# Two moves of work in program order in a two-layer hybrid backbone: gate-row fills one step sooner, and the opening of a seven-product FFN

## The chip, the cores and the metric

The kernel runs on one core of a Trainium2 chip. The metric is the device time of one execution in microseconds. Five engines matter here: PE (TensorE) multiplies matrices, DVE (VectorE) and ACT (ScalarE) do elementwise work, POOL (GpSimd) does slow elementwise work and fills, SP (SyncE) issues most DMAs. Each engine runs its own list of instructions in order; an instruction waits for semaphores of the others. All matrix work is fp32: each operand is split into a rounded high part and a low remainder, and each product is three matmuls (high by high, low by high, high by low).

## The reference

Two layers. Each has a mixing part and a feed-forward part on 512 latent tokens and, in layer 0, also on 256 context tokens (1024 channels):

```
z = modulate(x, norm1_g, sh1, sc1) @ w_in            # and the same for the context
au, av, bq, bk, bv, cq, ck, cv, co, cg = split_cols(z)
y_a = chunk_token_mlp(...); y_b = neighbourhood_attention(...)
h_lat, h_ctx = mlstm_bidirectional(lat_in, ctx_in, ctx_out)
x = x + g1 * (concat([y_a, y_b, h_lat * sigmoid(co)]) @ w_out)
x = x + g2 * swiglu(modulate(x, norm2_g, sh2, sc2), w_gate, w_up, w_down)
```

The mLSTM has an input gate `i` and a forget gate `f` per head, token and direction. Its running maximum and the cumulative sum of the forget gates are recurrences over tokens:

```
fcum = jnp.cumsum(fb, axis=-1)
log_intra = fcum[..., :, None] - fcum[..., None, :] + ib[..., None, :]
m_t = jnp.maximum(log_inter, jnp.max(log_intra, axis=-1))
```

## The kernel before, in words

**Mixing part.** The code of a layer is written as generators, one per strand of work: the attention head pairs B0 to B2, the mLSTM head pairs C0 to C2, the gate rows `r` (`do_Crows`, line 671), the values `v`, the modulation vectors `m`. A table of strings, `ORDERS`, says how many steps each generator takes and in what order; a step ends at a `yield`. The framework then places the emitted instructions into one list per engine, so that program order and its view of readiness set the lists; they are fixed before the program starts. In layer 0 the gate rows stand as `r:1 m:1 C0:1 r:2`: the first step of `do_Crows`, a step of modulation, a step of C0, then two more steps of `do_Crows`.

The first step of `do_Crows` spreads the gates into two padded tiles, transposes them on PE (`rowps`) and copies them out on ACT as rows `rI` and `rF` (64 partitions by 768 tokens). The second step fills two more row tiles on POOL, `rM` with 0 (line 701) and `rW` with 1 and two strips of zeros (lines 709 to 711), and runs three DVE scans that write the running maximum into `rM` (line 717). The third step runs two more scans, with `rW` as the multiplier (line 721), and a subtraction into `rI`. The fourth subtracts into `rF` (line 729), forms `rW`, `rA` and `apr`, and takes their exponentials on ACT (lines 738 to 744). Then PE transposes the rows back (`tokps`, line 759) and broadcasts `apr` (`apbps`).

Around it stand the rope products of the mLSTM (`th`, `ck`, `cq`, lines 785 to 796, with one multiply on POOL at 794), the triangular masks `s_tri` on POOL (line 850), and the large projections (`dps`, line 157), whose weights arrive by DMA as `wraw` and are split into `whi` on ACT (line 133) and `wlo` on DVE (line 134).

**Opening of layer 0's FFN.** Up and gate projections of the first layer are done by a scheme of seven products in place of eight half-size ones (`ffn_seven`, line 1417). A unit is one block of gate or up weights. The products are P1 and P2 (weights as they are), P6 and P5 (weight sums `s2`, `s1`), P7 and P4 (`b`), P3 (`s4`). Their right-hand operands are built from pairs j = 0..3 of normalised rows `hf`: P1 and P2 use `hf` itself; P6 and P5 use T2 and T1, two subtractions (`sums_12`, lines 1228 and 1229, tiles `t`) and then a split into high and low (`operands_12`, line 113 on ACT, line 114 on DVE; tiles `olh` and `oll` for j = 0, `oh` and `ol` for the others); T3, T4 and B22 come from `operands_34`. `some_steps(n)` normalises n more rows (line 1189 on DVE, line 1191 on ACT). The first two units run side by side with their operands being built, so this place is called the opening. `w1`, `w2`, `w3`, `w4` split a unit's weights (tiles `whi`, `wlo`); `X`, `Y`, `Z` are its PSUM banks (line 1314). `pin` fixes the order of the PE products as written.

Of the kernel before, what the change touches and what calls it, by code (L numbers as in the profile page):

```python
# [46 lines left out]
def tile_backbone(ctx: ExitStack, tc: tile.TileContext, A, out):  # L47
    nc = tc.nc
    te, ve, ac, gp, sp = nc.tensor, nc.vector, nc.scalar, nc.gpsimd, nc.sync
# [47 lines left out]
    def pst(pool, name="ps"):  # L97
        return pool.tile([128, 512], F32, tag="ps", name=name)
# [7 lines left out]
    def zct(name, dt=F32):  # L106
        return zc.tile([128, ZU], dt, tag="z", name=name)
# [19 lines left out]
    def wload(src):  # L127
        n = src.shape[-1]
        raw = wraw.tile([128, 1024], F32, tag="w", name="wraw")
        link(sp.dma_start(out=raw[:, 0:n], in_=src))  # L130
        hi = whl.tile([128, 1024], F32R, tag="whi", name="whi")
        lo = whl.tile([128, 1024], F32R, tag="wlo", name="wlo")
        ac.activation(out=hi[:, 0:n], in_=raw[:, 0:n], func=AF.Copy)  # L133
        ve.tensor_tensor(out=lo[:, 0:n], in0=raw[:, 0:n], in1=hi[:, 0:n].bitcast(F32), op=ALU.subtract)  # L134
        return hi, lo
# [318 lines left out]
    for l in range(2):  # L454
# [216 lines left out]
        def do_Crows():  # L671
# [13 lines left out]
            ve.tensor_scalar(out=f64v, in0=gt[:, :, :, 1, :], scalar1=0.0, scalar2=None, op0=ALU.min)  # L685
            ve.tensor_tensor(out=f64v, in0=f64v, in1=fa, op=ALU.subtract)

            def to_rows(src, name):
                t = zct(name)
                for g, (c0, n) in enumerate(((0, 4), (4, 2))):  # L690
                    ps = pst(mx, "rowps")
                    for c in range(n):
                        te.transpose(out=ps[0:64, c * 128:(c + 1) * 128], in_=src[:, c0 + c, :], identity=ident)
                    ac.activation(out=t[0:64, c0 * 128:(c0 + n) * 128], in_=ps[0:64, 0:n * 128], func=AF.Copy)
                return t
# [1 line left out]
            rI = to_rows(i64, "rI")  # L697
            rF = to_rows(f64, "rF")
            yield
            rM = zct("rM")  # L700
            gp.memset(rM[0:64, 0:768], 0.0)
            mst = tok.tile([64, 6], F32, tag="mst", name="mst")
            gp.memset(mst, 0.0)
            mla = tok.tile([64, 6], F32, tag="mla", name="mla")
            gp.memset(mla, 0.0)

            rW, rA = zct("rW"), zct("rA")
            keep = rW[0:64, 0:768].rearrange("p (c t) -> p c t", c=6)
            gp.memset(rW[0:64, 0:768], 1.0)
            gp.memset(keep[0:32, :, 0], 0.0)  # L710
            gp.memset(keep[32:64, :, 127], 0.0)
            rM3 = rM[:, 0:768].rearrange("p (c t) -> p c t", c=6)
            runs = (
                (slice(0, 6), slice(0, 768, 1), 0.0), (slice(32, 38), slice(255, None, -1), 0.0),
# [15 lines left out]
            rM, rE = rF, rM  # L730
# [466 lines left out]
        def some_steps(n):  # L1197
            for _ in range(min(n, len(steps2))):
                steps2.pop(0)()
# [4 lines left out]
        def pair_tile(wide):  # L1204
            if wide:
                t = zct("t")
                return [t[:, n1], t[:, n2]], [t[:, 0:2 * HN]]
            t = [wkt("t")[:, 0:HN] for _ in range(2)]
            return t, t

        def round_off(names, j, srcs, dst):
            hi, lo = dst
            c = 0
            for src in srcs:
                q = slice(c, c + src.shape[-1])
                split(hi[:, q], lo[:, q], src)
                c += src.shape[-1]
            for i, nm in enumerate(names):
                q = slice(i * HN, (i + 1) * HN)
                O[nm, j] = (hi[:, q], lo[:, q])  # L1220

        def out_pair():
            return [zct(nm, F32R)[:, 0:2 * HN] for nm in ("oh", "ol")]

        def sums_12(j):
            e, o = hf[2 * j], hf[2 * j + 1]
            t, _ = tsum[j] = pair_tile(j < 3)
            ve.tensor_tensor(out=t[0], in0=e[:, n2], in1=e[:, n1], op=ALU.subtract)
            ve.tensor_tensor(out=t[1], in0=o[:, n2], in1=t[0], op=ALU.subtract)

        def operands_12(j):
            dst = [O["l"][w][:, 8:10, :].rearrange("p a b -> p (a b)") for w in (0, 1)] if j == 0 else out_pair()
            round_off(("T1", "T2"), j, tsum[j][1], dst)
# [161 lines left out]
        def feed(n):  # L1395
            for _ in range(min(n, len(fill))):
                fill.pop(0)()

        units, first = [], []
# [17 lines left out]
        def ffn_seven():  # L1417

            def down(pi):
                f0, nf = FF0_PIECES[pi]  # L1420
                gh, gl = [], []
                for pr in range(f0 // 2, (f0 + nf) // 2):
                    gh += store[pr][0]
                    gl += store[pr][1]

                def gpart(g):
                    o, T = (0, 512) if g[0] == "l" else (512, 256)
                    return (lambda k: gh[k][:, o:o + T], lambda k: gl[k][:, o:o + T], T)

                cache = {}  # L1430

                def dload(k):
                    if k // 4 not in cache:
                        cache[k // 4] = wload(A["w_dn0_%d" % pi][k // 4])
                    c = (k % 4) * nf * 128
                    return [t[:, c:c + nf * 128] for t in cache[k // 4]]

                return nf, gpart, dload

            u0, u1 = first  # L1440

            some_steps(2)
            sums_12(0)
            for j in range(1, 4):
                for u in first:
                    u.prod("P1", u.X, [j])
                if j == 3:
                    for u in first:
                        u.snap1()
                for u in first:  # L1450
                    u.prod("P2", u.Y, [j])
            for u in first:
                u.w2()
                u.Z = pst(mx, "Z")
            units[2].w1()
            for j in range(4):
                if j < 3:
                    some_steps(2)
                    sums_12(j + 1)
                operands_12(j)  # L1460
                for nm, at in (("P6", "X"), ("P5", "Z")):
                    for u in first:
                        u.prod(nm, getattr(u, at), [j], start=(nm == "P5"))
            for j in range(4):
                operands_34(j)
                if j == 1:
                    u0.fin1()
                    for u in first:
                        u.snap2()
                    for u in first:  # L1470
                        u.snap5()
            u1.fin1()
            units[2].stage1(True)
            for u in first:
                u.w3()
            for u in first:
                u.prod("P7", u.X, start=False)
                u.fin22()
            u0.stage3()
            u1.stage3()  # L1480
            units[2].sums()
            units[2].w2()
            units[2].fin1()
            units[2].stage2a()
            nu = 2
            for pi in range(len(FF0_PIECES)):
                nf = FF0_PIECES[pi][1]
                if pi:
                    for i in range(nf):
                        u = units[nu + i]  # L1490
                        if i:
                            u.stage2a()
                        u.stage2b()
                        feed(1)
                        nxt = units[nu + i + 1] if nu + i + 1 < len(units) else None
                        if nxt is not None:
                            nxt.stage1()
                            nxt.sums()
                            nxt.w2()
                        u.stage3(nxt is None)  # L1500
                        if nxt is not None:
                            nxt.fin1()
                    if nxt is not None:
                        nxt.stage2a()
                    nu += nf
                nf, gpart, dload = down(pi)
                pin_d[0] = pin[0]
                if pi < len(FF0_PIECES) - 1:
                    for k in range(KD):
                        resid(dense(dload(k), nf, [gpart(g) for g in whole], mm if k % 2 == 0 else mx), k, 5, whole)  # L1510
                        if k % 4 == 1:
                            feed(1)
                    pin[0] = last_pe[0]
                else:
                    feed(len(fill))

                    def done(g, ssq):
                        norm1_begin(1, h_next, x, groups.index(g), ssq)

                    preload(AF.Sqrt)  # L1520
                    lagged(dload, nf, gpart, 5, done, *TRAIL[1], eng=ve)
# [19 lines left out]
        for pi, (f0, nf) in enumerate(FF_PIECES):  # L1541
# [32 lines left out]
            def dload(k):  # L1574
                return wload(A["w_down%d" % pi][l, k])
# [120 lines left out]
```

## Time and profile before

| what | value |
|---|---|
| median of 3 runs | 1675.41 us (1675.05 to 1676.37) |
| profiled execution: its own time | 1679.51 us |
| profiled execution: span | 1677.5 us, mean granted PE clock 0.987 |
| PE busy | 1608.3 us (96%) |
| DVE busy | 1109.3 us (66%) |
| ACT busy | 736.0 us (44%) |
| POOL busy | 150.0 us (9%) |

Times in the rows of the trace are microseconds from the start of the span. A row of the timeline has the start, the duration, the engine, the line, the operation, output from inputs, the shape and the count; a bracket at its end gives the idle time of that engine before the row, and what ended it. Durations of matmuls overlap: the distance from one start to the next is what PE spends on one. Buffer numbers are left out of the names.

### The profile page before, as it was taken

How to read it: one execution, taken by the hardware profiler on the slowest of the kernel's cores; microseconds unless marked ns; L12 is line 12 of the kernel's file. 1: busy time of each engine (PE TensorE's matmuls, PEld its weight loads, DVE VectorE, ACT ScalarE, POOL GpSimd, SP SyncE). 2: the span in 40 equal slices, each digit the busy share in tenths (PEclk: the TensorE clock that was granted, in tenths of full speed). 3: DMA queues.
4: the chain of work that ended last, by engine and by line, in shares of the span. 5: the costliest groups of instructions: out<-in, count | busy, mean ns of one | idle time of the engine just before them, and what ended most of it. 6: DMA issues, size and time to landing. Idle time of an engine off the chain costs nothing.

```text
span 1677.5 us, 26358 instructions
## 1 busy us (share of the span) xinstructions
PE 1608.3 (96%) x10536; PEld 1413.3 (84%) x10536; DVE 1109.3 (66%) x1945; ACT 736.0 (44%) x1366; POOL 150.0 (9%) x183
## 2 busy tenths in 40 slices
PE   7998998999889999999999999899989999999998
PEld 6876877878889999999999979687869988888888
DVE  4587777667887787778777774854687833333335
ACT  5564544763563333333333454545744432222235
POOL 0003013022100000000000000130143000000000
PEclk9998999999999999999999999999999999999999
DMA  8752323244223333333333323111256532323222
GB/s 305 256 164 83 103 84 98 64 136 141 76 61 107 109 113 126 114 126 121 106 126 111 122 80 117 35 64 50 71 182 196 184 122 97 101 90 99 101 71 87
DMA packets 59306, 192.91 MB, mean 115 GB/s; under 512 B 7088, under 2 KB 9008, under 8 KB 59056
## 3 DMA queue, kind: packets, MB, share of 16 engines
q1 hardware_dynamic: 53424, 170.26, 30.8%
q0 software_dynamic: 5760, 20.97, 4.1%
q8 instruction: 83, 1.36, 0.3%
q14 instruction: 39, 0.32, 0.1%
HBM read 183.87 MB, written 7.34 MB: 114 GB/s over the span
## 4 chain that ended last, share of the span: by engine, by line
PE 75%; DVE 14%; ACT 4%; DMA 3%; issue 3%; POOL 1%; DVEq 0%; SPq 0%; ACTq 0%; POOLq 0%
PE dps L157 43%; PE X L1314 10%; PE Z L1314 5%; PE wps L413 4%; PE vps L659 3%; PE Y L1314 2%; DMA wmod<-in_w_mod 2%; DVE wlo L134 2%; DVE wmod L223 1%; PE bops L553 1%; DVE junk L223 1%; PE ptps L595 1%; ACT prob L583 1%; PE bsps L553 1%; PE avps L990 1%
## 5 line engine op out<-in xcount | busy, mean ns | idle before, releaser
L133 ACT ACTIVATE whi<-wraw 128x1024 fp32r<-128x1024 f32 (+2 forms) x178 | 180.9, 1017 | 342.8 <-PE dps L157 224.3
L134 DVE TENSOR_TENSOR wlo<-wraw,whi 128x1024 fp32r<-128x1024 f32 (+2 forms) x178 | 211.2, 1187 | 130.7 <-ACT whi L133 116.3
L1126 DVE SCALAR_TENSOR_TENSOR x<-dps,modT,x 128x512 f32<-128x512 f32 (+1 forms) x240 | 137.6, 602 | 84.1 <-PE dps L157 79.6
L157 PE MATMUL dps<-gh,whi 128*128 128x512 f32 (+1 forms) x576 | 171.4, 343 | 1.8 <-DVE x L1126 1.7
L157 PE MATMUL dps<-gl,whi 128*128 128x512 f32 (+1 forms) x576 | 170.6, 342 | 0.8 <-DVE gl L114 0.8
L157 PE MATMUL dps<-gh,wlo 128*128 128x512 f32 (+1 forms) x576 | 170.5, 341 | 0.0
L223 DVE SCALAR_TENSOR_TENSOR wmod<-wmod,c_all 128x1024 f32<-128x1024 f32 x96 | 120.9, 1260 | 29.3 <-DMA wmod<-in_w_mod 28.9
L157 PE MATMUL dps<-ll,whi 128*128 128x512 f32 x336 | 135.7, 404 | 0.2 <-DVE ll L114 0.2
L157 PE MATMUL dps<-lh,wlo 128*128 128x512 f32 x336 | 135.3, 403 | 0.0
L157 PE MATMUL dps<-lh,whi 128*128 128x512 f32 x336 | 134.8, 402 | 0.0
L157 PE MATMUL dps<-h2lh,whi 128*128 128x512 f32 (+1 forms) x336 | 128.0, 384 | 0.0
L157 PE MATMUL dps<-h2ll,whi 128*128 128x512 f32 (+1 forms) x336 | 128.0, 384 | 0.0
L157 PE MATMUL dps<-h2lh,wlo 128*128 128x512 f32 (+1 forms) x336 | 127.9, 384 | 0.0
L157 PEld LDWEIGHTS dps<-gh,whi 128*128 128x128 f32 x576 | 98.4, 189 | 16.5 <-DVE x L1126 2.9
L157 PEld LDWEIGHTS dps<-gl,whi 128*128 128x128 f32 x576 | 97.4, 188 | 15.2 <-DVE gl L114 1.9
L157 PEld LDWEIGHTS dps<-gh,wlo 128*128 128x128 f32 x576 | 97.4, 188 | 13.4
L113 ACT ACTIVATE whi<-s 128x512 fp32r<-128x512 f32 x66 | 39.4, 627 | 102.8 <-PE dps L157 75.5
L157 PE MATMUL dps<-ch,whi 128*128 128x256 f32 x256 | 74.9, 292 | 8.5 <-ACT bv L528 5.4
L113 ACT ACTIVATE whi<-wraw 128x1024 fp32r<-128x1024 f32 x44 | 46.4, 1055 | 74.1 <-PE dps L157 68.0
L157 PE MATMUL dps<-ch,wlo 128*128 128x256 f32 x256 | 74.4, 291 | 2.9 <-DVE wlo L134 2.9
L157 PEld LDWEIGHTS dps<-lh,whi 128*128 128x128 f32 x336 | 64.2, 191 | 14.7 <-issue 1.3
L157 PEld LDWEIGHTS dps<-ll,whi 128*128 128x128 f32 x336 | 64.2, 191 | 14.5 <-issue 1.7
(408 smaller groups left out, 3884.5 us busy)
## 6 DMA issues: line engine op xcount, KB each, us to landing
wmod<-in_w_mod SPq DMA_DIRECT2D x56, 512.0 KB, 3.7
wraw<-in_w_seven SPq DMA_DIRECT2D x44, 512.0 KB, 3.3
wmod<-in_w_mod POOLq DMA_DIRECT2D x40, 512.0 KB, 3.8
wraw<-in_win_blk SPq DMA_DIRECT2D x34, 512.0 KB, 3.6
wraw<-in_w_out SPq DMA_DIRECT2D x23, 512.0 KB, 3.4
wraw<-in_w_dn SPq DMA_DIRECT2D x22, 512.0 KB, 3.3
wraw<-in_w_up SPq DMA_DIRECT2D x21, 512.0 KB, 3.3
wraw<-in_w_gate SPq DMA_DIRECT2D x20, 512.0 KB, 3.3
```

What stands on the lines that cost most here:

```text
L113: ac.activation(out=hi, in_=src, func=AF.Copy)
L133: ac.activation(out=hi[:, 0:n], in_=raw[:, 0:n], func=AF.Copy)
L134: ve.tensor_tensor(out=lo[:, 0:n], in0=raw[:, 0:n], in1=hi[:, 0:n].bitcast(F32), op=ALU.subtract)
L157: m = te.matmul(out=ps[:, 0:T], lhsT=wt[:, c], rhs=(flo if wh else fhi)(k), start=(k == 0 and wi == 0), stop=(k == nk - 1 and wi == 2),)
L223: ve.scalar_tensor_tensor(out=wraw.tile([128, D], F32, tag="w", name="junk") if t < ts[-1] else raw, in0=raw, scalar=1.0, in1=c_all[:, t, ...
L413: m = te.matmul(out=ps[:, 0:T], lhsT=wt[:, cs_], rhs=(flo if wh else fhi)(k), start=(k == 0 and wi == 0), stop=(k == KD - 1 and wi == 2))
L553: m = te.matmul(*args, **kw)
L583: ac.activation(out=pt[:, 0:n], in_=sps[:, 0:n], func=AF.Exp, bias=nm, accum_out=sm_)
L595: te.transpose(out=tps[:, i * 128:(i + 1) * 128], in_=pt[:, i * 128:(i + 1) * 128], identity=ident)
L659: te.matmul(out=vps[i][:, 0:408], lhsT=tokslice(nm, k, i), rhs=wt[:, cs], start=(k == 0 and wi == 0), stop=(k == KD - 1 and wi == 2))
L1126: ve.scalar_tensor_tensor(out=xs, in0=ps, scalar=modT[:, row * 8 + k, g[3]:g[3] + 1], in1=xs, op0=ALU.mult, op1=ALU.add)
L1314: m = te.matmul(out=ps[:, 0:HN], lhsT=wt[:, c], rhs=O[op, j][wh], start=(start and j == 0 and wi == 0), stop=(j == 3 and wi == 2), skip_gr ...
```

## The change

In `do_Crows` the tiles `rM` and `rW` are allocated and filled on POOL before the first `yield`, thus in the first step instead of the second. In `ffn_seven`, T1 and T2 of pair 0 are written ahead of the weight-sum splits of the first two units; rows 2 and 3 and the subtractions of pair 1 move up with them. The split of the third unit's plain weights moves from before the loop to its pass j = 2.

```diff
             ve.tensor_tensor(out=f64v, in0=f64v, in1=fa, op=ALU.subtract)
 
+            rM = zct("rM")
+            gp.memset(rM[0:64, 0:768], 0.0)
+            rW = zct("rW")
+            keep = rW[0:64, 0:768].rearrange("p (c t) -> p c t", c=6)
+            gp.memset(rW[0:64, 0:768], 1.0)
+            gp.memset(keep[0:32, :, 0], 0.0)
+            gp.memset(keep[32:64, :, 127], 0.0)
+
             def to_rows(src, name):
...
             yield
-            rM = zct("rM")
-            gp.memset(rM[0:64, 0:768], 0.0)
             mst = tok.tile([64, 6], F32, tag="mst", name="mst")
...
-            rW, rA = zct("rW"), zct("rA")
-            keep = rW[0:64, 0:768].rearrange("p (c t) -> p c t", c=6)
-            gp.memset(rW[0:64, 0:768], 1.0)
-            gp.memset(keep[0:32, :, 0], 0.0)
-            gp.memset(keep[32:64, :, 127], 0.0)
+            rA = zct("rA")
...
                 for u in first:
                     u.prod("P2", u.Y, [j])
+            some_steps(2)
+            sums_12(1)
+            operands_12(0)
             for u in first:
                 u.w2()
                 u.Z = pst(mx, "Z")
-            units[2].w1()
             for j in range(4):
-                if j < 3:
+                if 0 < j < 3:
                     some_steps(2)
                     sums_12(j + 1)
-                operands_12(j)
+                if j:
+                    operands_12(j)
+                if j == 2:
+                    units[2].w1()
                 for nm, at in (("P6", "X"), ("P5", "Z")):
```

No instruction is added or dropped; the lists of the engines change at three places: the gate rows of layer 0, the opening, and the gate rows of layer 1. Line numbers of the changed kernel are larger by 2 behind line 721, and by 7 behind the FFN's opening.

POOL at the gate rows of layer 0 (`f` is the padded forget-gate tile, `th` the rope product, `s_tri` and `s_sb` the masks). Before:

```order
L677 MEMSET f_1238 128x384
L794 ISA
L794 TENSOR_TENSOR th<-th,cst 128x512 x2
L850 AFFINE_SELECT s_tri<-s_sb 128x768 x2
L701 MEMSET rM 64x768
L709 MEMSET rW 64x768
L850 AFFINE_SELECT s_sb<-s_sb 128x768
L710 MEMSET rW 32x6
L711 MEMSET rW 32x6
```

With the change:

```order
L677 MEMSET f_1238 128x384
L689 MEMSET rM 64x768
L692 MEMSET rW 64x768
L693 MEMSET rW 32x6
L694 MEMSET rW 32x6
L796 ISA
L796 TENSOR_TENSOR th<-th,cst 128x512 x2
L852 AFFINE_SELECT s_tri<-s_sb 128x768 x2
L852 AFFINE_SELECT s_sb<-s_sb 128x768 x2
```

The four fills stand directly behind the fill of `f`, ahead of both rope products and all masks.

DVE in the opening, from the subtractions of pair 0 (`t_4864`) on; `wlo_4908` and `wlo_4915`, with the change `wlo_4917` and `wlo_4924`, are the low halves of the two units' weight sums, `wlo_4926` is that of the third unit. Before:

```order
L1228 TENSOR_TENSOR t_4864<-hf_4542 128x384
L1189 SCALAR_TENSOR_TENSOR hf_4544<-x2_4148,a2_230,rb_4858 128x256
L1229 TENSOR_TENSOR t_4864<-hf_4543,t_4864 128x384
L1189 SCALAR_TENSOR_TENSOR hf_4545<-x3_4149,a2_230,rb_4858 128x256
L1189 SCALAR_TENSOR_TENSOR hf_4546<-x4_4150,a2_230,rb_4858 128x256
L114 TENSOR_TENSOR wlo_4915<-s2_4829,whi_4914 128x512
L114 TENSOR_TENSOR wlo_4915<-s1_4828,whi_4914 128x512
L114 TENSOR_TENSOR wlo_4926<-wraw_4921,whi_4925 128x1024
L1228 TENSOR_TENSOR t_4933<-hf_4544 128x384
L114 TENSOR_TENSOR oll_4541<-t_4864,olh_4540 128x768
```

With the change:

```order
L1230 TENSOR_TENSOR t_4864<-hf_4542 128x384
L1191 SCALAR_TENSOR_TENSOR hf_4545<-x3_4149,a2_230,rb_4858 128x256
L1231 TENSOR_TENSOR t_4864<-hf_4543,t_4864 128x384
L1230 TENSOR_TENSOR t_4911<-hf_4544 128x384
L114 TENSOR_TENSOR wlo_4917<-s1_4821,whi_4916 128x512
L1231 TENSOR_TENSOR t_4911<-hf_4545,t_4911 128x384
L114 TENSOR_TENSOR oll_4541<-t_4864,olh_4540 128x768
L114 TENSOR_TENSOR wlo_4924<-s2_4829,whi_4923 128x512
L114 TENSOR_TENSOR wlo_4924<-s1_4828,whi_4923 128x512
L1191 SCALAR_TENSOR_TENSOR hf_4546<-x4_4150,a2_230,rb_4858 128x256
```

The split `oll` of pair 0 now stands ahead of the second unit's low halves; the third unit's low half has left this place and follows the split of pair 2. On ACT, `olh` moves likewise ahead of the second unit's two high halves and of the third unit's.

DVE at the gate rows of layer 1; `wlo_10657` is the low half of a projection's weights, `th` and `cq` belong to the rope products, `rM`, `rF`, `rI`, `rW`, `rA` are the gate rows. Before, from that split to the first scan of 768 tokens:

```order
L580 TENSOR_REDUCE nm_10422<-bsps_10413 128x1
L134 TENSOR_TENSOR wlo_10657<-wraw_10654,whi_10656 128x1024
L584 RECIPROCAL sum_10425<-sum_10425 128x1
L580 TENSOR_REDUCE nm_10430<-bsps_10414 128x1
L584 RECIPROCAL sum_10433<-sum_10433 128x1
L791 SCALAR_TENSOR_TENSOR cq_9869<-th_10471,cq_9869 128x512
L793 STREAM_SHUFFLE th_10471<-cq_9869 128x512
L785 SCALAR_TENSOR_TENSOR cq_10283<-dps_10484,small_673,cq_10283 128x511
L795 TENSOR_TENSOR cq_9869<-cq_9869,cst_96 128x512
L787 SCALAR_TENSOR_TENSOR cq_10283<-dps_10484,small_673,cq_10283 128x511
L796 TENSOR_TENSOR cq_9869<-th_10471,cq_9869 128x512
L717 SCALAR_TENSOR_TENSOR rM_10519<-rF_10378,rI_10367 6x768
```

With the change, from the subtraction into `rI` (the scans stand ahead of it) to that split:

```order
L729 TENSOR_TENSOR rI_10373<-rI_10373,rF_10384 64x768
L795 STREAM_SHUFFLE th_10518<-cq_10283 128x512
L731 TENSOR_TENSOR rF_10384<-rM_10367,rF_10384 64x768
L797 TENSOR_TENSOR cq_10283<-cq_10283,cst_96 128x512
L734 COPY mla_10527<-rF_10384 6x6
L735 COPY mla_10527<-rF_10384 6x6
L798 TENSOR_TENSOR cq_10283<-th_10518,cq_10283 128x512
L739 TENSOR_TENSOR rW_10369<-rF_10384,mst_10525 64x768
L741 TENSOR_TENSOR rA_10529<-rI_10373,mla_10527 64x768
L745 TENSOR_TENSOR apr_10548<-mst_10525,mla_10527 64x6
L134 TENSOR_TENSOR wlo_10657<-wraw_10654,whi_10656 128x1024
```

Before, the split stood ahead of all scans; now it stands behind the whole chain of gate rows, and the scans of 768 tokens stand ahead of the rope products of `cq`.

## The prediction

> **What bounds the kernel now.** I read the page first, its busy shares and its chain of waits, then the list of PE's waits, then windows around the longest waits inside the changed places, then the rows there.
>
> ```profile
> PE 1608.3 (96%) x10536; PEld 1413.3 (84%) x10536; DVE 1109.3 (66%) x1945; ACT 736.0 (44%) x1366; POOL 150.0 (9%) x183
> PE 75%; DVE 14%; ACT 4%; DMA 3%; issue 3%; POOL 1%; DVEq 0%; SPq 0%; ACTq 0%; POOLq 0%
> PE dps L157 <- ACT bv L528: 5.4, 1, 5.4
> PE tokps L759 <- DVE rI L727: 5.1, 1, 5.1
> PE X L1314 <- ACT olh L113: 3.0, 1, 3.0
> ```
>
> PE is busy for 96% and carries 75% of the chain: the time moves only where PE stops waiting or runs faster. Of its waits (total, number, longest), the second, third and seventh largest totals lie in the three places whose lists change. A wait costs more than itself, as the granted clock shows (columns: window; PE busy, PEld, DVE, ACT, POOL; clock; DMA share; GB/s):
>
> ```profile
> 122.00:166.00 44.00, 36.82 (x279) 30.97 (x279) 34.33 (x65) 23.19 (x52) 11.80 (x16) 0.91 0.23 70
> 152.00:157.00 5.00, 4.61 (x18) 4.36 (x19) 4.93 (x13) 4.67 (x11) 0.14 (x2) 0.50 0.36 107
> 166.00:203.00 37.00, 36.94 (x300) 30.92 (x300) 25.75 (x54) 17.21 (x45) 1.07 (x2) 0.97 0.34 105
> 462.00:468.00 6.00, 5.28 (x15) 4.88 (x16) 6.00 (x13) 4.81 (x10) 0.00 (x0) 0.50 0.00 0
> 468.00:500.00 32.00, 28.94 (x157) 27.03 (x157) 28.06 (x49) 19.75 (x34) 1.67 (x3) 0.99 0.18 52
> 1091.00:1096.00 5.00, 5.00 (x19) 4.23 (x18) 4.92 (x9) 2.85 (x5) 0.00 (x0) 0.50 0.54 160
> ```
>
> After each of the three long waits PE runs at half clock for 5 to 6 us, which loses some 2.6 us more. Which gap brings that on? Rows with gaps between:
>
> ```profile
> 439.34 0.39 PE L157 MATMUL dps<-ch,wlo 128*128 128x256 f32 x1 [1.74 <-DVE wlo L134]
> 437.00:444.00 7.00, 4.01 (x29) 3.60 (x30) 7.00 (x10) 6.43 (x12) 2.01 (x3) 1.00 0.21 75
> 255.68 0.45 PE L870 MATMUL ups<-av,kt 128*64 128x65 f32 x8 [2.32 <-POOL av L843]
> 260.00:264.00 4.00, 4.00 (x15) 3.38 (x15) 1.91 (x5) 2.94 (x12) 1.42 (x3) 0.54 0.06 25
> 1225.52 1.47 PE L827 MATMUL sps<-cq,ck 64*128 64x128 f32 x16 [3.22 <-DVE cq L796]
> 1225.00:1230.00 5.00, 4.48 (x28) 4.05 (x29) 5.00 (x6) 2.56 (x5) 5.00 (x5) 0.66 0.25 77
> ```
>
> A gap of 1.74 us, with two smaller ones near it, left the clock at 1.00. A gap of 2.32 us (and a shorter one behind it) and one of 3.22 us halved it.
>
> **Layer 0's gate rows.** The fills cost the same wherever they stand; the term is what waits for them.
>
> ```profile
> 136.81 2.28 POOL L850 TENSOR_SCALAR_AFFINE_SELECT s_tri<-s_sb 128x768 f32<-128x768 f32 x2 [3.65 <-ACT s_sb L836]
> 139.04 0.73 POOL L701 MEMSET rM<- 64x768 f32 x1
> 139.80 2.97 DVE L717 TENSOR_TENSOR_SCAN rM<-rF,rI 6x768 f32<-6x768 f32 x2 [2.25 <-POOL rM L701]
> 149.98 0.94 DVE L729 TENSOR_TENSOR rF<-rM,rF 64x768 f32<-64x768 f32 x1
> 151.02 0.84 ACT L741 ACTIVATE rM<-rM 64x768 f32<-64x768 f32 x1 [0.30 <-DVE rF L729]
> 151.77 0.57 ACT L528 ACTIVATE bv<-dps 128x512 f32<-128x512 f32 x1
> 152.39 0.58 PE L157 MATMUL dps<-ch,whi 128*128 128x256 f32 x1 [5.36 <-ACT bv L528]
> 129.75 0.85 ACT L694 ACTIVATE rF<-rowps 64x512 f32<-64x512 f32 x2
> 130.53 0.74 DVE L793 STREAM_SHUFFLE th<-cq 128x512 f32<-128x512 f32 x1
> ```
>
> The chain is: masks, fill, scans, subtraction into rF, exponential of rM on ACT; bv stands behind that exponential in ACT's list, and PE waits for bv. With the fills standing far ahead, the scans wait only for rF's copy (129.75 + 0.85) and for the shuffle ahead of them on DVE (130.53 + 0.74): they start at about 131.3, 8.5 us sooner. Walking the new DVE list with these durations (three scans 4.2, two scans 3.5, two rope operations 1.3 and one weight split 1.2 among them, rI's subtraction 0.9) brings rF's subtraction to 143.1 in place of 149.98; rM's exponential starts there.
>
> What is late next: ACT's new list has rM's exponential, two softmax exponentials with their read-outs, rW's exponential and only then the scaled probabilities. They are ready at about 146.5, and PE, with the products ahead of their transposes (ptps) done, is there at 143.4: a wait of 3.1 us. Three smaller waits come on the way: 0.85 for the rows rF (1.52 before), 1.25 for a rope addition of ck that now stands behind a reciprocal, and 0.5 at bops. Waits before, 122 to 166: 1.52 + 0.23 + 5.36 = 7.1; after: 0.85 + 1.25 + 0.5 + 3.1 = 5.7. That gains 1.4. Half clock before cost 2.65 (152.39 to 157.7) and again about 0.95 at 165.9 to 167.8, together 3.6. If the gap of 3.1 halves the clock again (2.6 lost, as behind the 3.05 and the 5.36), the place gains 1.4 + 3.6 − 2.6 = 2.4; if not, 5.0. Being nearest to the gaps of 3.05 and 3.22, it most likely does, though the stretch behind 3.22 was shorter, some 4 us with 2 lost: I take **2.7** of 2.4 to 5.0. The rope of cq and the weight split that slip behind the scans are hidden: that weight's products start long after 142.2, where its low half lands. Without that cover they would cost up to their 1.2.
>
> The Trainium skill, page "TensorE: Matmul & The Clock Gate", section "Part 1: The HAM clock gate", says that the clock halves after at least one idle window of about 3.4 us, the windows running freely. By that no gap of about 3 us would halve it, and the place would gain the 5.0. The rows above speak against it (3.05, 3.22 halved); it enters as a rival.
>
> **The opening.** Now:
>
> ```profile
> 459.54 1.28 DVE L114 TENSOR_TENSOR wlo<-s,whi 128x512 fp32r<-128x512 f32 x2
> 460.80 1.22 DVE L114 TENSOR_TENSOR wlo<-wraw,whi 128x1024 fp32r<-128x1024 f32 x1
> 461.46 0.83 ACT L113 ACTIVATE olh<-t 128x768 fp32r<-128x768 f32 x1
> 462.41 0.95 DVE L114 TENSOR_TENSOR oll<-t,olh 128x768 fp32r<-128x768 f32 x1
> 465.01 0.95 DVE L114 TENSOR_TENSOR ol<-t,oh 128x768 fp32r<-128x768 f32 x1
> 462.35 0.69 PE L1314 MATMUL X<-olh,whi 128*128 128x384 f32 x1 [3.05 <-ACT olh L113]
> 463.41 0.69 PE L1314 MATMUL X<-oll,whi 128*128 128x384 f32 x1 [0.38 <-DVE oll L114]
> 475.80 0.96 DVE L114 TENSOR_TENSOR ol<-t,oh 128x768 fp32r<-128x768 f32 x1 [1.08 <-ACT oh L113]
> 478.08 1.21 DVE L114 TENSOR_TENSOR wlo<-wraw,whi 128x1024 fp32r<-128x1024 f32 x1
> 484.17 0.44 PE L1314 MATMUL X<-oh,wlo 128*128 128x384 f32 x1 [1.10 <-DVE wlo L114]
> ```
>
> PE waits 3.05 for olh, which stands on ACT behind two units' splits, then 0.38 for oll, then runs at half clock to 468.4. With the splits behind it, olh starts once pair 0's subtractions are done (one at 458.1 in the new list), at 459.0, and ends at 459.8; oll ends at about 461.0. So pair 0 starts 2.4 us sooner. But DVE is never idle from 443 to 473, and moving rows does not make it shorter: its new list gives ol of pair 1 a start at 464.65 (465.01 before), of pair 2 at 466.0 (467.68), of pair 3 at 468.5. PE's pair 0 (12 products, 0.174 each) is over at 463.1, and PE waits about 2.5 us in two pieces for pair 1. Then it follows, pair 3 ending at about 471.9 in place of 474.0.
>
> Late next: ACT takes the banks Z, then a third-stage weight's high half, then the oh that DVE awaited for 1.08 at 475.80. All this moves up by some 0.6 to 1.5, so DVE loses most of its 1.08 wait, and the low half at 478.08, for which PE waits behind it, lands about 0.9 sooner. From there to the end of the opening DVE works 28.06 of 32 us and each PE wait (the 1.10 at 484.17 the largest) is for DVE, so both keep the shift. Bounds: none, if PE halves its clock again here and pair 3 ends where it did; 2.1, if all of pair 3's lead survives. The gaps (0.7, 1.0, 1.4, 1.1) are of the size of those at 437 to 444 that left the clock alone. I take **0.9**. The third unit's split, two passes later, costs nothing: its first products stand behind pair 3 and all six later waits; ahead of pair 3's ol, it takes the 1.14 that the earlier place gives back.
>
> **Layer 1's gate rows.**
>
> ```profile
> 1065.42 1.79 DVE L795 TENSOR_TENSOR ck<-ck,cst 128x512 f32<-128x512 f32 x1
> 1078.27 1.74 DVE L717 TENSOR_TENSOR_SCAN rM<-rF,rI 6x768 f32<-6x768 f32 x1
> 1089.54 0.95 DVE L727 TENSOR_TENSOR rI<-rI,rF 64x768 f32<-64x768 f32 x1
> 1090.55 0.90 PE L759 MATMUL tokps<-cst,rI 64*128 64x64 f32 x6 [5.13 <-DVE rI L727]
> ```
>
> Here too the scans move up, into DVE's idle time at 1061 to 1064 and behind it, and rI ends at about 1083.3 in place of 1090.5. PE's list has tokps six products earlier, so it comes there at 1080.4 and waits 2.95. But the split wlo_10657, which was done at 1071.7, now stands behind rA and apr and lands at about 1089.9; PE has six high-half products ready (1.2) and then waits some 3 us for it. From 1089.9: two products 0.35, two groups of tokps 0.8, apbps 1.4, then 43 products of 0.231 and 21 of 0.12, 12.4: 1105.0, where before was 1106.36. At full clock the gain is 1.4. With half clock behind the second gap, 2.6 lost, it is −1.2. Between, because the half-clock stretch behind the first gap falls mostly into the second wait and costs nothing there: **0.5**.
>
> **Sum.** 2.7 + 0.9 + 0.5 = 4.1. From the profiled execution, 1679.51 (span 1677.5 and 2.0 around it), that is 1675.4; it stands 4.1 above the median shown, 1675.41, so the changed kernel's median would be **1671.3**. What lies between the places stays as it is: PE has no wait to speak of from 166 to 203 (36.94 of 37), none worth naming from 500 to 950, and the waits at 227 to 260 follow work that shifts along. A difference under 0.2%, 3.35 us, is not told from no change here.
>
> **The rivals.** (1) *The waits only move* (0.28): layer 0 keeps its gain of 1.4 in waits, but the half clock comes back in both places, and the opening stays bound by DVE: 2.4 + 0.4 − 1.2 = 1.6, 1673.8. For: new gaps of 2.95 to 3.1 in place of old of 5.1 to 5.4; DVE without slack in the opening. Against: 255.68 is the shortest gap with that effect, and layer 1's first gap is mostly covered.
> (2) *No new half clock* (0.2): 5.0 + 1.3 + 1.4 = 7.7, 1667.7. The window that the Trainium skill's page states would give this; the 3.05 and 3.22 rows speak against it, the 1.74 for gaps that come out shorter than I walked.
> (3) *The late low half makes it slower* (0.12): in layer 1, wlo_10657 behind the gate chain decides PE. It breaks even when it lands at 1091.3; rope operations next to POOL's multiply take up to 1.79 (at 1065.42) where one alone in layer 0 took 0.69, and several of them stand ahead of it, so it can land at 1093, costing 1.7, and with half clock 2.6 more: −4.3. If the same pushing back of rope work behind scans makes layer 0's masks late (sps is released by cq, as at 1225.52, waiting 3.22), its 2.7 goes as well: with the opening's 0.9 the sum is −3.4, 1678.8.
> (4) *The change does not reach PE* (0.05): other rows on DVE hold the scans; 0, 1675.4.
>
> **How the numbers follow.** My forecast has 0.35, with a range of its own from 1669.5 to 1673. Range: 1666.8 (rival 2 with 0.9 more) to 1677.2 (rival 3 by half its distance), leaving about 2 in 10 outside. Faster by over 3.35: most of the forecast (0.25 of 0.35), rival 2 (0.2) and some of rival 1 (0.07): 0.52. Slower by over 3.35: rival 3, 0.12. Within: 0.36.
>
> **What would show it.** Right: POOL's fills ahead of its rope product in both layers; scans in layer 0 at 131 to 132; PE's wait for bv gone and one of about 3 for prob at ptps, half clock behind it; in the opening olh near 459.0, PE waiting at pair 1 instead of pair 0; in layer 1 a wait for rI near 3 and one for wlo_10657. Wrong: scans of layer 0 later than 135, a wait for bv or cq over 3, layer 1's trps later than 1106.4 less the shift ahead of it, or a clock below 0.9 in 462 to 468.

## The result, and the profile after

| kernel | median | ratio to before (95% interval) |
|---|---|---|
| before, timed beside it | 1676.37 us (1675.05 to 1678.03, 5 runs) | |
| changed | 1684.63 us (1682.81 to 1689.69, 5 runs) | 1.0053 (1.0042 to 1.0065) |
| changed, timed once more (e5 below) | 1684.13 us, before 1677.76 us | 1.0040 (1.0027 to 1.0054) |

The change makes the kernel slower by some 6 to 9 us. The forecast was 1671.3 us, with a range up to 1677.2: sign and size were wrong. One of the twelve executions of e2 below ran at a granted clock of 0.556 and took 2595.02 us; e2's figures leave it out.

The busy row of the changed kernel's page (span 1681.8 us, own time 1684.63):

```profile
PE 1609.5 (96%) x10536; PEld 1413.3 (84%) x10536; DVE 1112.4 (66%) x1945; ACT 734.7 (44%) x1366; POOL 150.9 (9%) x183
```

The two rows of its list of PE's waits that answer to those of before (total, number, longest):

```profile
PE ptps L595 <- ACT prob L585: 10.5, 7, 5.5
...
PE tokps L761 <- DVE rI L729: 3.5, 1, 3.5
```

The three old waits are gone from the top or shorter: bv no longer stands there, rI went from 5.1 to 3.5. In their place ptps waits 10.5 us in seven waits for the scaled probabilities (4.3 in five before). To see where time is lost, the same product is found in both profiled executions and its starts are compared (`sps` is a product of the mLSTM that needs the rope product of `cq`; `ptps` and `trps` are transposes):

| PE's product, place | before, us | changed, us | shift |
|---|---|---|---|
| first ptps in attention's second pair, layer 0 | 97.67 | 97.36 | −0.3 |
| sps, in the gate rows of layer 0 | 134.18 | 136.96 | +2.8 |
| last product Y ahead of the opening | 458.96 | 462.68 | +3.7 |
| first dps behind the opening | 499.15 | 501.56 | +2.4 |
| tail of layer 0's FFN (last Z) | 950.79 | 951.78 | +1.0 |
| trps behind the gate rows of layer 1 | 1106.36 | 1109.40 | +3.0 |

So layer 0 lost, the opening gained 1.3, and layer 1 lost. Part of the first loss is a half clock at 99 to 102 that the change did not touch (last section), and the FFN between 502 and 951 took 449.6 to 452.5 us from one profile to another with the same PE list, so single profiles tell the place, not the amount to a microsecond; the amounts come from timed experiments.

**Layer 0.** Rows of the changed kernel's timeline around the gate rows, of POOL, of DVE, of ACT and of PE:

```profile
132.44 3.20 POOL L796 TENSOR_TENSOR th<-th,cst 128x512 f32<-128x512 f32 x1 [9.81 <-ACT kt L818]
142.88 1.67 POOL L852 TENSOR_SCALAR_AFFINE_SELECT s_sb<-s_sb 128x768 f32<-128x768 f32 x2
132.17 1.73 DVE L719 TENSOR_TENSOR_SCAN rM<-rF,rI 6x768 f32<-6x768 f32 x1
134.51 1.67 DVE L719 TENSOR_TENSOR_SCAN rM<-rF,rI 6x256 f32<-6x256 f32 x1
138.25 4.01 DVE L723 TENSOR_TENSOR_SCAN rF<-rW,rF 6x768 f32<-6x768 f32 x2
142.29 0.65 DVE L725 COPY mst<-rM 6x5 f32<-6x5 f32 x1
142.95 0.80 DVE L726 COPY mst<-rM 6x3 f32<-6x3 f32 x1
143.90 1.46 DVE L729 TENSOR_TENSOR rI<-rI,rF 64x768 f32<-64x768 f32 x1
146.42 0.94 DVE L731 TENSOR_TENSOR rF<-rM,rF 64x768 f32<-64x768 f32 x1
147.45 0.84 ACT L743 ACTIVATE rM<-rM 64x768 f32<-64x768 f32 x1 [6.89 <-DVE rF L731]
150.49 0.89 ACT L585 ACTIVATE prob<-prob,sum 128x256 f32<-128x256 f32 x2
151.04 1.11 PE L595 MATMUL ptps<-cst,prob 128*128 128x128 f32 x4 [5.54 <-ACT prob L585]
179.49 0.66 PE L595 MATMUL ptps<-cst,prob 128*128 128x128 f32 x4 [0.67 <-ACT prob L585]
190.85 0.39 PE L157 MATMUL dps<-ch,whi 128*128 128x256 f32 x1 [0.76 <-ACT bk L528]
```

The scans do start 7.6 us sooner (132.17 for 139.80). But the subtraction into rF comes only 3.6 us sooner, and the probabilities behind its exponential make PE wait 5.54, as long as bv did. The windows (PE busy, PEld, DVE, ACT, POOL; clock; DMA share; GB/s) of the places whose windows of before stand in the prediction:

```profile
122.00:166.00 44.00, 35.88 (x281) 28.99 (x280) 36.88 (x68) 25.56 (x61) 13.43 (x14) 0.92 0.14 47
151.00:157.00 6.00, 5.96 (x18) 4.62 (x18) 3.91 (x6) 4.92 (x10) 0.00 (x0) 0.51 0.26 87
166.00:203.00 37.00, 35.51 (x296) 29.21 (x295) 22.32 (x43) 15.27 (x38) 0.00 (x0) 1.00 0.36 108
462.00:468.00 6.00, 3.66 (x18) 2.77 (x17) 6.00 (x13) 5.99 (x12) 0.00 (x0) 1.00 0.07 28
1085.00:1099.00 14.00, 11.17 (x45) 8.79 (x44) 10.29 (x13) 6.09 (x11) 3.46 (x4) 0.51 0.34 99
```

Half clock stands again behind the long wait, at 151 to 157, and at 166 to 203, where PE was busy 36.94 of 37 before, it is now 35.51: the two last PE rows above are new waits there.

**Layer 1.** PE's rows:

```profile
1083.46 0.56 PE L761 MATMUL tokps<-cst,rI 64*128 64x64 f32 x6 [3.46 <-DVE rI L729]
...
1087.28 0.58 PE L157 MATMUL dps<-ch,whi 128*128 128x256 f32 x1 [1.27 <-ACT bk L528]
...
1090.49 0.80 PE L157 MATMUL dps<-lh,wlo 128*128 128x512 f32 x1 [1.56 <-DVE wlo L134]
...
1092.77 2.67 PE L774 MATMUL apbps<-apr,selp 64*128 64x6 f32 x12
...
1109.40 0.81 PE L489 MATMUL trps<-cst,ck 128*128 128x128 f32 x6
```

Three waits follow each other, 3.46, 1.27 and 1.56, and the last row of the windows above shows the price: 14 us at half clock, against the 5 of before.

**The opening** answers to the forecast. PE's waits:

```profile
463.69 0.44 PE L1316 MATMUL X<-olh,whi 128*128 128x384 f32 x1 [0.67 <-ACT olh L113]
464.82 0.44 PE L1316 MATMUL X<-oll,whi 128*128 128x384 f32 x1 [0.69 <-DVE oll L114]
468.09 0.44 PE L1316 MATMUL X<-oh,whi 128*128 128x384 f32 x1 [1.08 <-ACT oh L113]
469.41 0.45 PE L1316 MATMUL X<-ol,whi 128*128 128x384 f32 x1 [0.88 <-DVE ol L114]
482.04 0.45 PE L1316 MATMUL X<-oh,wlo 128*128 128x384 f32 x1 [1.76 <-DVE wlo L114]
```

The wait of 3.05 at pair 0 became 0.67, pair 1 now waits 1.96 in two pieces, and the clock at 462 to 468 is 1.00.

### The profile page after: what moved, and what is told of

It is laid out like the page before. It is cut to its first block, busy times and chain, and to the rows that moved or that the text cites. A ratio compares the mean times of both kernels' runs of the same rounds, so it can differ in the third digit from the quotient of the medians.

```text
span 1681.8 us, 26366 instructions
## 1 busy us (share of the span) xinstructions
PE 1609.5 (96%) x10536; PEld 1413.3 (84%) x10536; DVE 1112.4 (66%) x1945; ACT 734.7 (44%) x1366; POOL 150.9 (9%) x183
## 4 chain that ended last, share of the span: by engine, by line
PE 75%; DVE 15%; ACT 5%; issue 2%; DMA 2%; POOL 1%; DVEq 0%; SPq 0%; ACTq 0%; POOLq 0%
PE dps L157 44%; PE X L1316 10%; PE Z L1316 5%; PE wps L413 4%; PE vps L659 3%; PE Y L1316 2%; DVE wlo L134 2%; DMA wmod<-in_w_mod 2%; DVE wmod L223 1%; PE bops L553 1%; DVE junk L223 1%; PE ptps L595 1%; ACT prob L583 1%; PE avps L992 1%; PE bsps L553 1%
## 5 line engine op out<-in xcount | busy, mean ns | idle before, releaser
L157 PEld LDWEIGHTS dps<-lh,wlo 128*128 128x128 f32 x336 | 64.3, 191 | 15.7 <-DVE wlo L134 2.3
```

Source lines behind the costliest of these rows:

```text
L157: m = te.matmul(out=ps[:, 0:T], lhsT=wt[:, c], rhs=(flo if wh else fhi)(k), start=(k == 0 and wi == 0), stop=(k == nk - 1 and wi == 2),)
```

## The experiments

Theory A: both moved gate rows cost time, each for a reason of its own place, and the opening gives a little back. Rivals: one of the two places alone carries the loss, or the opening does. Four kernels take the change apart.

**e1_rows_only**: the early fills in both layers, the opening as before.

```diff
+            rM = zct("rM")                        # in do_Crows, ahead of the first yield,
+            gp.memset(rM[0:64, 0:768], 0.0)       # with the fills of rW, as in the change
...
             for u in first:                       # in ffn_seven, as before
                 u.w2()
                 u.Z = pst(mx, "Z")
             units[2].w1()
```

> Only the early fills of rM and rW (both layers); the opening as before. Theory A (the gate rows lose: in layer 0 the scans now run beside GpSimd's rope multiply and masks and PE waits 5.5 us for prob; in layer 1 a weight split stands behind the whole gate chain and PE stays at half clock for some 13 us): 5 to 9 us slower than before. Theory B (chance half-clock stretches elsewhere make the difference): within 1.5 us of before in the median. Theory C (the opening is what loses): 4 us faster, as forecast for the rows.

Measured: 1684.98 us beside 1677.96, ratio 1.0044 (1.0032 to 1.0056). Within the intervals the whole loss stands in the gate rows.

**e2_opening_only**: the change's hunk in ffn_seven alone, the fills as before.

```diff
+            some_steps(2)
+            sums_12(1)
+            operands_12(0)
             for u in first:
...
-            units[2].w1()
...
+                if j == 2:
+                    units[2].w1()
```

> Only the changed opening; the gate rows as before. Theory A: 0.5 to 2 us faster than before, with PE waiting less than 1 us for olh and no half clock at 459 to 470. Theory B: within 1.5 us of before. Theory C: 4 to 9 us slower.

Measured: 1678.92 us beside 1677.96, ratio 1.000 (0.999 to 1.0011). No gain that can be told. From the last Y ahead of the opening to the first dps behind it, profiles of kernels with the old opening show 40.0 to 40.6 us (seven of them); with the new one 38.9 in three (changed, e2, e10) and 40.6 to 40.7 in three others (e5, e6, e7). The last section shows the clock that goes with it.

**e3_rows_layer0** and **e4_rows_layer1**: the early fills in one layer only, the opening as before.

```diff
+            if not last:          # e3; e4 has: if last
+                rM = zct("rM")
+                gp.memset(rM[0:64, 0:768], 0.0)
...
             yield
+            if last:              # e3; e4 has: if not last
+                rM = zct("rM")
...
```

> Early fills in layer 0 alone. Theory A: 1.5 to 4 us slower than before, with a wait of 5 us or more for prob at ptps and half clock behind it. Forecast as it was made: 2.7 us faster. Theory B: within 1.5 us.

> Early fills in layer 1 alone. Theory A: 2.5 to 5 us slower than before, half clock from about 1083 to 1099. Forecast as it was made: 0.5 us faster; its slower rival: 1.7 to 4.3 slower. Theory B: within 1.5 us.

Measured: e3 1680.60 us, 1.0016 (1.0006 to 1.0025); e4 1681.13 us, 1.0022 (1.0013 to 1.0032), both beside 1677.96. By the ratios layer 0 loses about 2.7 us and layer 1 about 3.7, together 6.4, where e1 lost 7.4 with an interval of 5.4 to 9.4. No rival holds. Layer 1's chain alone, PE's rows of e4:

```profile
1083.97 0.87 PE L772 MATMUL tokps<-cst,rI 64*128 64x64 f32 x6 [3.46 <-DVE rI L740]
...
1093.26 2.67 PE L785 MATMUL apbps<-apr,selp 64*128 64x6 f32 x12
```

And the window behind that wait:

```profile
1087.00:1099.00 12.00, 10.58 (x42) 8.21 (x41) 8.79 (x13) 5.55 (x11) 2.50 (x3) 0.50 0.34 99
```

The wait is the same 3.46, and the half clock about as long.

**e5_change_again**: the changed kernel once more, beside the next three.

> The changed kernel once more, beside the two that are built on it, on the same chip. Theory A (two mechanisms in the gate rows, layer 0 and layer 1): 6 to 9 us slower than before, as e1. Theory B (chance half-clock stretches): anything within 3 us.

Measured: 1.0040 (1.0027 to 1.0054).

**e6_masks_late**: does POOL's work beside the scans make rF late? Layer 0's first masks are emitted one step later; in the lists only POOL's four mask rows move.

```diff
-            s_tri = [[masked(su, zct("s_tri"), 0) for su in s_sb], None]
+            late = p == 0 and not last
+            if not late:
+                s_tri = [[masked(su, zct("s_tri"), 0) for su in s_sb], None]
             yield
+            if late:
+                s_tri = [[masked(su, zct("s_tri"), 0) for su in s_sb], None]
```

> The changed kernel, but layer 0's first masks (GpSimd, line 852) are written one step later, so that GpSimd does them after the scans; nothing else moves on any engine. Theory A1 (the scans run slow because GpSimd's masks run beside them): the two scans into rF take 3.5 us again in place of 4.0, the copies mst 0.15 each in place of 0.65 and 0.80, rI's subtraction 0.95 in place of 1.46; PE's wait for prob at ptps falls by some 2 us and the time by 1 to 3 us against the changed kernel. Theory A2 (only the order of the lists counts): no change in the scans and the wait.

Rows of e6, DVE, then PE:

```profile
138.74 3.52 DVE L723 TENSOR_TENSOR_SCAN rF<-rW,rF 6x768 f32<-6x768 f32 x2
142.29 0.16 DVE L725 COPY mst<-rM 6x5 f32<-6x5 f32 x1
142.46 0.16 DVE L726 COPY mst<-rM 6x3 f32<-6x3 f32 x1
142.77 0.95 DVE L729 TENSOR_TENSOR rI<-rI,rF 64x768 f32<-64x768 f32 x1
144.78 0.94 DVE L731 TENSOR_TENSOR rF<-rM,rF 64x768 f32<-64x768 f32 x1
149.40 0.84 PE L595 MATMUL ptps<-cst,prob 128*128 128x128 f32 x4 [2.58 <-ACT prob L585]
```

With no mask beside them the two scans take 3.52 in place of 4.01, the copies 0.16 in place of 0.65 and 0.80, rI's subtraction 0.95 in place of 1.46, and PE's wait falls from 5.54 to 2.58. That POOL's masks stretched the chain is shown. In the profiles the move gives back layer 0's loss: from PE's arrival at the rowps of 126 us to its arrival at the product of layer 0's tail that waits 0.57 for whi (last section), the five profiles with layer 0's fills early, the masks and the softmax in their old places, show 313.4 to 315.2 us, the six with the fills late 307.6 to 310.3, and e6 shows 310.7. In the time it does not show: 1684.71 us, 1.0035 (1.0021 to 1.0049), against 1.0040 of e5, with five executions of each. So what part of layer 0's timed loss the masks carry stays open, and even without them the early fills win nothing in that one profile of the stretch.

**e7_split_first_l1**: is layer 1's loss the order in which the weight split, the gate chain and PE's tokps stand? One word of the changed kernel's table moves.

```diff
-    ("B0:1 C1:1 B0:1 v:2 B0:2 v:1 B0:1 C0:1 r:1 B0:1 C1:1 C0:1 r:4 B1:1 C0:3 ...
+    ("B0:1 C1:1 B0:1 v:2 B0:2 v:1 B0:1 C0:1 r:1 B0:1 C1:1 C0:1 B1:1 r:4 C0:3 ...
```

> The changed kernel, but in layer 1 the step of the attention pair B1 that holds the late weight split is written ahead of the gate rows' last four steps. The split then stands among the scans on DVE, not behind the chain. Theory A (the late split starves PE and keeps it at half clock): the half clock from 1083 to 1099 is gone or short, and the time is 3 to 7 us below the changed kernel. Theory A3 (layer 1 loses because rI itself is late and tokps waits for it): the wait for rI stays near 3.5 and the time within 1.5 us of the changed kernel.

Measured: 1672.45 us beside 1677.76, 0.9968 (0.9955 to 0.998): 11.7 us faster than the changed kernel timed beside it (1684.13), more than the 3 to 7 of theory A, and faster than before. The window of layer 1's gate rows in the kernel before:

```profile
1070.00:1111.00 41.00, 35.87 (x214) 29.85 (x213) 29.76 (x44) 17.11 (x35) 7.14 (x10) 0.92 0.23 71
```

In the changed kernel:

```profile
1070.00:1111.00 41.00, 34.71 (x182) 28.66 (x182) 26.88 (x39) 15.04 (x30) 5.61 (x5) 0.83 0.20 61
```

In e7:

```profile
1070.00:1111.00 41.00, 41.00 (x317) 33.93 (x318) 32.27 (x56) 20.06 (x45) 12.66 (x15) 1.00 0.25 74
```

Its row of tokps:

```profile
1096.49 0.59 PE L761 MATMUL tokps<-cst,rI 64*128 64x64 f32 x6
```

In e7 PE never stops in these 41 us and the clock stays at 1.00. The splits stand among the scans on DVE (`wlo` at 1073.26 and 1081.89 in place of 1089.22), and tokps stands later in PE's list: PE comes to it at 1096.5, where it came to it and waited at 1080.0 in the changed kernel. Of these 16.5 us 1.6 are e7's lag from earlier, so some 15 us of ready products stand ahead of tokps, and the gate chain is done when PE comes. The one word moves both, the split and tokps; no run moves the late split alone.

**e8_softmax_first_l0**: can the same be done in layer 0? Early fills in layer 0 alone, masks late as in e6, and the softmax put ahead of rF's subtraction on DVE and of the gate exponentials on ACT.

```diff
-  ... C0:1 r:2 B0:1 m:1 r:1 m:1 B0:2 r:1 C0:1 ...
+  ... C0:1 r:2 B0:1 m:1 m:1 B0:2 r:1 r:1 C0:1 ...
+            if not last:
+                after(i, soft[0])     # rF's subtraction behind the softmax's reciprocal
...
+            if not last:
+                after(i, soft[1])     # rE's exponential behind the scaled probabilities
```

> Early fills in layer 0 alone, masks late as in e6, and the softmax of the attention block ahead of the exponentials of the gate rows on ACT and ahead of rF's subtraction on DVE. Layer 1 and opening as before. Theory A (in layer 0 PE waits for prob because the gate rows' exponentials stand ahead of it): the wait of 5.5 at ptps falls below 2 us, and the kernel is 1 to 5 us faster than before. Rival: the wait turns up at tokps or at the masks, and the time is within 1.5 us of e3.

Measured: 1678.43 us, 1.0005 (0.9997 to 1.0014). By the ratios most of e3's loss (1.0016) is back, though the intervals overlap, but nothing is won, and neither expectation holds in full: ptps still waits 3.21 (5.50 in e3), and a new wait of 0.58 for POOL's av stands at 164. Late masks and the softmax's place are moved together here, so what each gives back is not told apart.

**e9_order_alone**: the kernel before with the word of e7 moved and nothing else.

```diff
-  ... C0:1 r:4 B1:1 C0:3 ...
+  ... C0:1 B1:1 r:4 C0:3 ...
```

**e10_l1_early_split_first_opening**: e9 with the early fills in layer 1 alone (as in e4) and the new opening (as in e2). **e11_l1_early_split_first**: e10 with the old opening, thus e9 and the fills alone.

```diff
-  ... C0:1 r:4 B1:1 C0:3 ...
+  ... C0:1 B1:1 r:4 C0:3 ...
+            if last:
+                rM = zct("rM")
...
+            some_steps(2)                         # e10 alone, with the rest of e2's hunk
```

> The kernel before with one word of layer 1's table moved, the projection's step ahead of the four gate-row steps; all fills late, opening as before. Theory A (what pays in layer 1 is where the weight split and tokps stand; the early fills only made the scans' start possible): the scans still stand behind POOL's late fill, but tokps stands later in PE's list, so that the 5.1 us wait for rI at 1090.5 shrinks to 0 to 2 us and its half clock goes: 3 to 6 us faster, ratio 0.9965 to 0.998. Theory B (the gain needs both, the early fills and the order): the gate chain ends as late as before and PE meets it at another product: within 1.5 us of the kernel before, ratio 0.999 to 1.001.

> Early fills in layer 1 alone, with the projection's step ahead of the gate-row steps there, and the changed opening; layer 0's fills as before. Theory A (layer 0's early fills cost 2.7 us wherever layer 1 stands): e7 less that loss, 0.9968 less 0.0016: 0.995 to 0.9957, some 7.5 us faster than before. Rival (the losses do not add; half clock falls elsewhere): the ratio of e7 again, 0.9955 to 0.998.

> As the kernel with early fills and the new order in layer 1 and the changed opening, but with the opening as before. Theory A (the opening is worth nothing that these times can tell, as timed alone at 1.000): within 0.001 of that kernel. Rival (the opening gains the 1.2 us that two profiles show): 0.0007 above it.

Measured, beside before at 1677.09: e9 1673.35 us, 0.998 (0.9971 to 0.9989); e10 1668.17 us, 0.9942 (0.993 to 0.9955); e11 1669.10 us, 0.995 (0.9938 to 0.9963). So the order alone gains 3.7; the early fills in layer 1, a loss of 3.7 in the old order, gain another 4 in the new one (e11 against e9); and layer 0's early fills, by which e7 differs from e10, cost about 4 (0.9968 against 0.9942; the 2.7 of e3 lies within these intervals). PE's rows of e9:

```profile
1091.70 0.58 PE L759 MATMUL tokps<-cst,rI 64*128 64x64 f32 x6
1093.80 0.58 PE L759 MATMUL tokps<-cst,rA 64*128 64x64 f32 x6 [1.51 <-ACT rA L740]
```

The windows of e9 behind that wait:

```profile
1095.00:1099.00 4.00, 4.00 (x20) 3.01 (x21) 3.03 (x4) 2.98 (x10) 1.64 (x3) 0.60 0.29 87
1099.00:1103.00 4.00, 4.00 (x37) 3.03 (x37) 0.00 (x0) 1.48 (x3) 2.12 (x5) 0.55 0.47 175
```

PE's rows of e10:

```profile
1092.27 0.59 PE L772 MATMUL tokps<-cst,rI 64*128 64x64 f32 x6
1092.69 0.54 PE L772 MATMUL tokps<-cst,rA 64*128 64x64 f32 x6
...
1093.44 1.45 PE L785 MATMUL apbps<-apr,selp 64*128 64x6 f32 x12
```

With the fills late (e9) the chain ends just too late: no wait for rI, but 1.51 for the exponential of rA, and half clock behind it. Theory A had the half clock gone; over 1070 to 1111 the clock is the 0.92 of before, and what e9 saves is waiting, 1.51 for 5.13. In the kernel before, the split was not late (done at 1071.7), so this gain is put down to tokps' place. With the fills early (e10) there is no wait at all. e10 is the best version found, 9 us under the kernel before. Whether its opening adds anything over e11 is not told apart, 1 us of medians with intervals that overlap.

## Why the prediction was wrong

**Layer 1, +0.5 forecast, −3.7 measured (e4).** The walk of DVE's list was right: rI at 1083.3 (1083.46), the low half at 1089.9 (it released PE at 1090.49). The step that failed is "because the half-clock stretch behind the first gap falls mostly into the second wait and costs nothing there". The waits were shorter than one clock stretch but came in a row, and the clock stayed at 0.51 from 1085 to 1099: apbps took 2.67 for the 1.4 of the sum, and from apbps to trps it was 16.6 us for 13.8. That is the 4.4 by which trps missed 1105.0 (1109.40): 0.6 in the low half, 1.1 in the products and tokps behind it, 2.8 from apbps on, each rounded. The lower bound named, −1.2, had the right side but priced one stretch of 5 us where 14 came.

**Layer 0, +2.7 forecast, −2.7 measured (e3).** The scans' start was right: 131.3 forecast, 132.17 with the 1.0 that the head had slipped. "Walking the new DVE list with these durations" failed. The durations came from rows where the rope product on POOL and two of the four masks were over when the scans began; moved ahead, the scans run beside the rope product, and what follows runs beside all four masks. Beyond the forecast rows: 0.5 for the short scan (1.67 for 1.17), 0.5 for the two scans into rF, 0.7 for the second copy (0.80 for 0.13), 0.5 for rI. rF's subtraction came at 146.42 for 143.1, 2.3 late beside the head's 1.0. A second slip lies behind it: the text let rM's exponential start at 143.1, where the subtraction of 0.94 only begins; it started at 147.45. So the probabilities were 4.5 later than forecast, PE itself 2.1, and the wait at ptps was 5.54 for 3.1; e6 shows it as 2.58 with the masks away. The trace of before had the sign. Its last two masks already ran beside the short scan (1.17, where layer 1 of the same trace has 0.68) and, the last of them from 142.50 to 143.43, beside the first copy (0.65, where e6 has 0.16):

```profile
140.41 1.82 POOL L850 TENSOR_SCALAR_AFFINE_SELECT s_sb<-s_sb 128x768 f32<-128x768 f32 x1
142.80 0.65 DVE L723 COPY mst<-rM 6x5 f32<-6x5 f32 x1
```

Two waits of 0.67 and 0.76 behind 166, where the text said that what lies between the places stays as it is, make up 1.4 more: with all named waits the place has 9.3, where 5.7 was forecast and 7.1 stood before. The half clock came as forecast, six us behind the long wait. By these rows the place loses 2.2 in waits and gets back 0.7 of the 3.6 that half clock cost before (2.9 at 151 to 157): −1.5, inside e3's interval of −1.0 to −4.2 us. What lies between −1.5 and −2.7 no row accounts for; the interval holds both.

**The opening, +0.9 forecast, 0 timed (−1.8 to +1.7).** Each step of the walk held: 0.67 for olh, 0.69 for oll, 1.96 in two pieces for pair 1 (2.5 forecast), 38.9 us in place of 40.2. What was wrong is that gaps of this size "left the clock alone": in three of the six profiles with the new opening they did not. A chance of one half on a gain of 1.3 is not far from the forecast, but it is no sure 0.9.

**The rivals.** Rival 3 had the sign and one of its two places: wlo in layer 1 late, and with half clock −4.3, against −3.7 measured. Its mechanism, rope operations beside POOL's multiply ahead of wlo, was not it: the low half landed within 0.6 of the walk, and the half clock did the rest. It also put layer 0's loss on masks late for cq, where cq cost 0.66. It had a chance of 0.12. Rival 2, no new half clock, is ruled out: it stood behind both places in the profiles of the changed kernel, and behind gaps of 2.58 and 1.51 in e6 and e9. What the list of signs gave as wrong, "layer 1's trps later than 1106.4 less the shift ahead of it", is what happened.

## What to carry to other kernels

A move that starts a chain sooner changes what runs beside it and in which order its end meets the other chains: durations from the old place hold only where the same engines are busy. Look first at where the consumer stands in its own list: one word of the table, which put some 15 us of ready products ahead of tokps and the weight split among the scans, turned the same early fills from a loss of 3.7 us into a gain. And price a row of short waits as one long stretch at half clock, as the 14 us of this case, not each by itself.

## What the runs showed of the hardware

**The same gaps halve the clock in one profile and not in another.** In layer 0's tail PE waits 0.57 and 1.74 us one behind the other. Rows of before:

```profile
437.09 0.39 PE L157 MATMUL dps<-ch,whi 128*128 128x256 f32 x1 [0.57 <-ACT whi L133]
...
439.34 0.39 PE L157 MATMUL dps<-ch,wlo 128*128 128x256 f32 x1 [1.74 <-DVE wlo L134]
```

Its window:

```profile
436.00:449.00 13.00, 9.53 (x76) 8.92 (x75) 13.00 (x18) 10.22 (x17) 4.58 (x5) 1.00 0.36 122
```

Rows of the changed kernel:

```profile
440.52 0.39 PE L157 MATMUL dps<-ch,whi 128*128 128x256 f32 x1 [0.56 <-ACT whi L133]
...
442.77 0.39 PE L157 MATMUL dps<-ch,wlo 128*128 128x256 f32 x1 [1.75 <-DVE wlo L134]
```

Its window:

```profile
436.00:449.00 13.00, 10.69 (x74) 10.28 (x74) 12.78 (x19) 12.21 (x23) 4.15 (x4) 0.87 0.20 61
```

Before, e2, e9 and e10 show 1.00 here; the nine other profiles show 0.87 or 0.88 with the same two waits. All seven with layer 0's fills early are among the nine, and two of the six with the fills late: whether that is chance, thirteen profiles do not tell. In time the lower clock costs nothing at this place: from the first of the two products to the last Y ahead of the opening it is 21.4 to 22.2 us in the nine and 21.4 to 22.4 in the four, with DVE busy 12.78 and 13.00 of the 13 us above. The prediction had taken the one clock of 1.00 as a sign that gaps of this size are safe. The opening is alike: waits of 0.66, 0.66, 1.07 and 0.88 in e5 and a clock of 0.86 at 470 to 482, the same four to 0.03 us and 1.00 in the changed kernel's own profile. At 97.4 a wait of 1.89 was followed by 0.66 over 98 to 103, one of 1.86 before by 1.00. The Trainium skill, page "TensorE: Matmul & The Clock Gate", section "Part 1: The HAM clock gate", says that the windows run freely, which would fit these pairs but is not shown by them. The same section of the Trainium skill says that the clock halves after at least one idle window of about 3.4 us; the profiles with the lower clock disagree, since no single gap in these pairs is as long.

**POOL beside DVE.** The scan of 6x256 took 1.67 beside POOL's rope product and 0.68 in e7's layer 1 without it, and that product took 3.20 for the 1.72 of before. The copies went up by 0.5 and 0.6 and rI by 0.5 beside the masks. The Trainium skill, page "SBUF — State Buffer", section "Who interferes with whom", says that a DVE instruction with two SBUF inputs contends with a GpSimd instruction that reads SBUF; the rows agree for the scans and for rI. The rope's own product at 133.82 took its usual 0.66 while POOL's row was open. One behind the other would fit all three rows: POOL's rope product takes 1.29 where it starts first (121.33 in this trace; DVE's product beside it, from 121.62, took 1.55 there), and 1.29 back from its end at 135.64 is 134.35, about where the product ends (134.48); 0.68 back from the short scan's end at 136.18 is 135.50, about where POOL's row ends. That is worked out from the ends of the rows and not shown by a run of its own.
